# SyncE's queue in written order in the first attention stage, and the first values behind both score groups

## The chip, the cores and the metric

The kernel runs on one core of a Trainium2 chip. Such a core has a matrix engine (TensorE, PE in the profile), a vector engine (VectorE, DVE), an activation engine (ScalarE, ACT), a general engine (GpSimd, POOL) and SyncE (SP), whose queue issues the data transfers (DMAs). The metric is the time of one execution in microseconds (us) of the device. The median of three runs of the kernel before is 627.55 us (627.46 to 628.74).

## The reference

One layer of a decoder block, for 512 tokens of width 1024 and 16 learned tokens ahead of them. Two attention branches with 16 heads each read the same normalised input `u`, and a gate merges them:

```python
h = concatenate([meta_tokens, x])            # 16 + 512 rows
u = rmsnorm(h, pre_norm_g)
proj = u @ w_in                              # cq, ckv, k_pe, z_mla, fq, fk, fv, f_logit, z_fox, gate_a, gate_b
# MLA: low-rank queries and keys, 64 dimensions without and 32 with rotary position
q = rmsnorm(cq) @ w_uq;  kv = rmsnorm(ckv) @ w_ukv
o_mla = causal_attention(concat(q_nope, rope(q_pe)), concat(k_nope, rope(k_pe)), v_mla)
# FoX: plain heads of 64, logits shifted by a running sum of log forget gates
cum = cumsum(log_sigmoid(f_logit + b))
o_fox = causal_attention(fq, fk, fv, logit[t, s] += cum[t] - cum[s])
y_mla = (o_mla * silu(z_mla)) @ w_br_mla;  y_fox = (o_fox * silu(z_fox)) @ w_br_fox
mixed = (sigmoid(gate_a) * y_mla + sigmoid(gate_b) * y_fox) @ w_out
out = h + rmsnorm(mixed, post_norm_g)        # the 16 learned rows dropped
```

## The kernel before, in words

**Arithmetic.** A product of float32 operands is made of three passes on TensorE: each operand is split into a high part (cast by ScalarE, `wh` for weights) and the rest (subtracted on GpSimd or VectorE, `wl`), and high by high, high by low and low by high are summed in PSUM. So a weight must be loaded (`wload`, L120, tile `wraw`), cast and subtracted (`wsplit`, L138) before its matmuls. `wraw`, `wh` and `wl` have three buffers each, used in turn.

**Stages.** After the projections of the front, 16 attention stages follow, two heads each: FoX and MLA in turn, for pairs of heads 0 to 7 (L752). Stage 0 is FoX of pair 0, stage 1 MLA of pair 0, stage 2 FoX of pair 1. In a stage (`attention`, L640):
- `scores` (L661) makes the score matmuls into PSUM tiles `st`; there are four such banks (L475). Group 0 is the query blocks 0 to 2, group 1 is block 3. For each part VectorE adds the mask and takes the minimum (L683, out to `sf`), which also frees the bank.
- the exponentials run on ScalarE (L693), the sums and their reciprocals on VectorE (L702, L703).
- `norm` (L698) writes the probabilities as two float16 parts into `pn` (ScalarE L721, VectorE L722, GpSimd L708 to L713) and has SyncE transpose them by DMA into `pt` (L729): one transposition per block and head, of 3, 5, 7 and 9 tiles of 128.
- `values` (L734) multiplies the transposed probabilities with the values: two matmuls with `vm`, 24 with `vp`, into the tile `ov`. The first one for a head reads a part of `pt` that all four transpositions of this head write. The values of a stage are made one stage later, between that stage's score groups (`late`, L826).

**Fill.** Between these, TensorE does projections ("fills", L779 to L795): in stage 0 the gates `z` of FoX and MLA and the queries, keys and values of MLA; in stage 1 the next FoX queries `fq`, the rotary parts `ppe` of the second half of the heads, the keys `fk` and the values `v` of pair 1.

**What sets the order.** TensorE runs the attention part in the order in which it is written. In the first part of stage 0 (L808) ScalarE, VectorE and GpSimd do so too. SyncE's queue and all the rest are ordered by a scheduler when the program is built. SyncE issues one DMA after the other, and one that has to wait holds up those behind it. A unit's `make` (L199) splits its weights and asks for the loads of the next three units. The loads of stage 0 that matter here, by their names in the two programs: `fq` weights (832 before, 834 after), `ppe` weights (839, 841), `fk` weights (887, 953), FoX values' weights of pair 1 (1194, 1025), the gate `z` of stage 2 (1265, 1270). Among them stand the writing of rotated queries to DRAM (`qpe_dram`, L566) and their reading back as `QP` (L507), which waits for those writes and which the MLA scores of stage 1 need; and `CT` (L280), the forget sums for the FoX scores of the next pair.

## Time and profile before

| | before |
|---|---|
| median of 3 runs | 627.55 us |
| the profiled execution: its time | 627.48 us |
| its span, first to last instruction | 625.1 us |
| TensorE busy | 601.1 us (96%) |
| VectorE, ScalarE, GpSimd busy | 380.8, 384.7, 188.9 us |
| mean granted TensorE clock | 0.992 |
| DMA engines, time that packets took | 53.7% of 16 engines' span |

All times of the trace are counted from the start of the span. A row of a timeline has start and duration in us, the engine, the line of the kernel, the operation, the tiles out<-in, the shapes and a count; in square brackets stands how long the engine was idle before it and what ended that. "SPq" is SyncE's queue; a DMA's row there is the time that its issue took, not that of the transfer.

### The profile page before, as it was taken

The page shows a single profiled execution, that of the slowest core. Times are in us where ns is not written, and L with a number is a line of the kernel's source. Part 1 is how long each engine was busy: PE and PEld are TensorE (multiplying, and loading weights), DVE is VectorE, ACT ScalarE, POOL GpSimd, SP SyncE. Part 2 cuts the span into 40 slices and gives each one's busy share as a digit, 9 for nine tenths or more (in the row PEclk, how much of TensorE's full clock was granted, in tenths as well). Part 3 has the DMA queues.
Part 4 walks back from the last instruction along what each step waited for, and adds up shares of the span by engine and source line. Part 5 has one row for each costly group of instructions (what it writes and reads, how often), then busy time and mean ns, then how long its engine had stood idle before and what let it go on. Part 6 is the DMA issues. An engine that isn't in the chain of part 4 may idle for free.

```text
span 625.1 us, 11556 instructions
## 1 busy us (share of the span) xinstructions
PE 601.1 (96%) x4058; PEld 494.2 (79%) x4058; DVE 380.8 (61%) x1015; ACT 384.7 (62%) x838; POOL 188.9 (30%) x237
## 2 busy tenths in 40 slices
PE   3999997999999999999999999999999999999996
PEld 2879775988988989889889889887888875565885
DVE  3756566376477466565674773785977775655134
ACT  5746657388478477575774784786767754443421
POOL 3324632744425343353343444330000000003700
PEclk9999997999999999999999999999999999999998
DMA  8443577756647677557477467657253128333302
GB/s 280 130 84 91 102 164 171 187 139 152 167 109 168 164 130 149 140 138 182 102 166 180 103 159 150 159 140 201 73 157 97 46 70 266 104 102 101 102 34 102
DMA packets 204865, 85.40 MB, mean 137 GB/s; under 512 B 122684, under 2 KB 197820, under 8 KB 204808
## 3 DMA queue, kind: packets, MB, share of 16 engines
q1 hardware_dynamic: 204808, 84.67, 53.7%
q8 instruction: 32, 0.52, 0.3%
q14 instruction: 25, 0.20, 0.1%
HBM read 55.21 MB, written 4.26 MB: 95 GB/s over the span
## 4 chain that ended last, share of the span: by engine, by line
PE 92%; DVE 2%; ACT 2%; DMA 2%; SPq 1%; issue 0%; DVEq 0%; ACTq 0%
PE pg L92 14%; PE z L92 14%; PE v L92 8%; PE st L92 8%; PE fk L92 8%; PE po L92 7%; PE fq L92 7%; PE py L92 6%; PE ov L92 5%; PE yx L92 3%; PE psm L92 3%; PE mq L92 2%; PE yy L92 2%; PE vt L95 1%; PE mk L92 1%; DMA wsr<-in_w_in_dram 1%
## 5 line engine op out<-in xcount | busy, mean ns | idle before, releaser
L118 POOL TENSOR_TENSOR wl<-wraw,wh 128x1024 fp32r<-128x1024 f32 (+1 forms) x60 | 132.9, 2219 | 298.7 <-ACT wh L142 284.3
L142 ACT CAST wh<-wraw 128x1024 fp32r<-128x1024 f32 (+1 forms) x74 | 72.9, 986 | 88.0 <-issue 41.4
L693 ACT ACTIVATE sf<-sf,nb 128x144 f32<-128x144 f32 (+3 forms) x128 | 71.9, 565 | 6.1 <-DVE nb L683 6.1
L721 ACT ACTIVATE pn<-sf,ri 128x128 f16<-128x128 f32 (+3 forms) x128 | 61.9, 551 | 15.1 <-ACT sf L693 14.2
L722 DVE SCALAR_TENSOR_TENSOR pn<-sf,ri,pn 128x128 f16<-128x128 f32 (+3 forms) x128 | 65.7, 553 | 7.6 <-ACT pn L721 7.6
L92 PE MATMUL pg<-uTh,wh 128*128 128x512 f32 x128 | 51.9, 406 | 0.0
L92 PE MATMUL z<-uTh,wh 128*128 128x512 f32 x128 | 50.9, 398 | 0.0
L92 PE MATMUL z<-uTh,wl 128*128 128x512 f32 x128 | 50.1, 391 | 0.0
L92 PE MATMUL z<-uTl,wh 128*128 128x512 f32 x128 | 50.0, 391 | 0.0
L92 PE MATMUL pg<-uTh,wl 128*128 128x512 f32 x128 | 50.0, 391 | 0.0
L92 PE MATMUL pg<-uTl,wh 128*128 128x512 f32 x128 | 49.9, 390 | 0.0
L92 PE MATMUL st<-hlk,hlq 64*128 64x272 f32 (+3 forms) x480 | 48.3, 309 | 0.4 <-DVE nb L683 0.3
L683 DVE CUSTOM_DVE_ANT_0 sf<-st,maskt 128x272 f32<-128x272 f32 (+2 forms) x128 | 48.5, 435 | 0.1
L92 PE MATMUL py<-g,yw 128*128 128x512 f16 x192 | 42.6, 379 | 0.6 <-DVE yw L979 0.6
L92 PEld LDWEIGHTS st<-hlk,hlq 64*128 64x128 f32 x480 | 35.7, 187 | 6.8 <-ACT wh L142 2.5
L708 POOL TENSOR_TENSOR mt<-sf,ri 128x96 f32<-128x96 f32 (+1 forms) x32 | 9.5, 297 | 90.7 <-DVE ri L703 53.5
L92 PE MATMUL fk<-uTl,wh 128*128 128x256 f32 (+1 forms) x128 | 36.5, 285 | 0.0
L92 PE MATMUL v<-uTh,wh 128*128 128x256 f32 (+1 forms) x128 | 36.5, 285 | 0.0
L92 PE MATMUL fk<-uTh,wh 128*128 128x256 f32 (+1 forms) x128 | 36.5, 285 | 0.0
L92 PE MATMUL fk<-uTh,wl 128*128 128x256 f32 (+1 forms) x128 | 36.5, 285 | 0.0
L92 PE MATMUL v<-uTl,wh 128*128 128x256 f32 (+1 forms) x128 | 36.4, 285 | 0.0
L92 PE MATMUL v<-uTh,wl 128*128 128x256 f32 (+1 forms) x128 | 36.4, 284 | 0.0
(291 smaller groups left out, 1513.1 us busy)
## 6 DMA issues: line engine op xcount, KB each, us to landing
wraw<-in_w_in_dram SPq DMA_DIRECT2D x56, 512.0 KB, 4.5
yraw<-in_w_br_fox_dram SPq DMA_DIRECT2D x8, 512.0 KB, 6.1
yraw<-in_w_br_mla_dram SPq DMA_DIRECT2D x8, 512.0 KB, 3.6
wraw<-in_w_out_dram SPq DMA_DIRECT2D x8, 512.0 KB, 3.5
qpe_dram<-gT SPq DMA_DIRECT2D x8, 256.0 KB
pt<-pn SPq DMA_TRANSPOSE x128, 2.7
QP<-qpe_dram SPq DMA_DIRECT2D x8, 256.0 KB, 2.9
xr<-in_x_dram SPq DMA_DIRECT2D x4, 512.0 KB
```

Source lines behind the costliest of these rows:

```text
L92: nc.tensor.matmul(*a, **k)
L95: nc.tensor.transpose(*a)
L118: eng.tensor_tensor(out=lo, in0=src, in1=f32(hi), op=ALU.subtract)
L142: nc.scalar.copy(wh[:, :n], raw[:, :n])
L683: nc.vector.tensor_tensor_reduce(out=sf_of(h, b)[:, c0 : c0 + w], in0=ps[h][:, o : o + w], in1=maskt[:, m0 : m0 + w], scale=-scale, scalar ...
L693: nc.scalar.activation(sf, sf, AF.Exp, bias=sums["nb"][:, h, b : b + 1], scale=-1.0, accum_out=sums["su"][:, h, b : b + 1])
L708: nc.gpsimd.tensor_tensor(out=mt, in0=src, in1=ri.unsqueeze(3).broadcast_to([128, 2, nb_, META]), op=ALU.mult)
L721: nc.scalar.activation(hi, sf, AF.Copy, scale=rib)
L722: nc.vector.scalar_tensor_tensor(out=lo, in0=sf, scalar=rib, in1=hi, op0=ALU.mult, op1=ALU.subtract)
```

## The change

`make` can hand its loads to a list, and in stage 0 the loads that `z` of MLA asks for go on the list `lo`. Its entries (the subtraction for the MLA `z` weights and the load of the `fk` weights) are called, with the load of `QP`, among the transpositions of stage 0 behind those of block 1, where before `QP` alone was called behind those of block 0. SyncE joins the engines that run in written order, for the whole of stage 0. The loads of `CT` for pair 1, and those of stage 1's weights that are not yet loaded, are written behind the last transposition of stage 0; the keys' unit of pair 1 no longer loads `CT`. And in stage 1 alone, the values of stage 0 come behind both score groups instead of between them. The work is the same.

```diff
--- before.py
+++ after.py
@@ -196,11 +196,15 @@
         st = {}
         out = []
 
-        def make(*a):
+        def make(eng=None, later=None):
             if "w" not in st:
-                st["w"] = getw(*a)
-                for load in getattr(out[0][1], "nxt", ()):
-                    load()
+                st["w"] = getw(eng, later) if eng else getw()
+                loads = getattr(out[0][1], "nxt", ())
+                if later is None:
+                    for load in loads:
+                        load()
+                else:
+                    later.extend(loads)
 
         for i, sl in enumerate(sls):
             n = sl.stop - sl.start
@@ -270,14 +274,17 @@
     def q_fox(pr):
         return unit(f"fq{pr}", win_w(O_FQ, pr), u_act, KD, REAL, hl_done(("q", 1, pr), S, S))
 
+    def load_ct(pr):
+        for h in range(2):
+            nc.sync.dma_start(f32(CT[64 * h : 64 * h + 2, :]), c_dram[:, 2 * pr + h, :])
+
     def k_fox(pr):
         halves = hl_done(("k", 1, pr), L, HALF)
 
         def done(i, ps):
             halves(i, ps)
-            if pr and i:
-                for h in range(2):
-                    nc.sync.dma_start(f32(CT[64 * h : 64 * h + 2, :]), c_dram[:, 2 * pr + h, :])
+            if pr > 1 and i:
+                load_ct(pr)
         return unit(f"fk{pr}", win_w(O_FK, pr), u_act, KD, ALLT, done)
 
 
@@ -722,7 +729,7 @@
                             nc.vector.scalar_tensor_tensor(out=lo, in0=sf, scalar=rib, in1=hi, op0=ALU.mult,
                                                            op1=ALU.subtract)
                     for b in GRP[g]:
-                        if b == 1:
+                        if b == 2:
                             mid()
                         for h in range(2):
                             t0 = PN_STEP * (b % 3)
@@ -805,33 +812,44 @@
             fill = fills[si]
             with ExitStack() as head:
                 if si == 0:
-                    head.enter_context(tc.manual_schedule(engines={E_.PE, E_.Pool, E_.Activation, E_.DVE}))
-                    za, q, zb = early
-                    turn, rest = rope0
-                    za.make()
-                    q.make()
-                    lo = []
-                    turn()
-                    s0()
-                    zb.make(nc.vector, lo)
-                    e0({(0, 1): lambda: rest(1), (1, 1): lambda: rest(0)})
-                    s1()
-                    n0(lambda: load_qp(0))
-                    lo[0]()
-                    e1()
-                    run(fill[:4])
+                    head.enter_context(tc.manual_schedule(engines={E_.PE, E_.SP}))
+                    with tc.manual_schedule(engines={E_.PE, E_.SP, E_.Pool, E_.Activation, E_.DVE}):
+                        za, q, zb = early
+                        turn, rest = rope0
+                        za.make()
+                        q.make()
+                        lo = []
+                        turn()
+                        s0()
+                        zb.make(nc.vector, lo)
+                        e0({(0, 1): lambda: rest(1), (1, 1): lambda: rest(0)})
+                        s1()
+
+                        def between():
+                            load_qp(0)
+                            for fn in lo:
+                                fn()
+                        n0(between)
+                        e1()
+                        run(fill[:4])
                 else:
                     s0()
                     e0()
-                    for fn in late:
+                    for fn in late * (si > 1):
                         fn()
                     s1()
                     e1()
+                    for fn in late * (si == 1):
+                        fn()
                     run(fill[:4])
                     n0()
-            run(fill[4:11])
-            n1()
-            run(fill[11:])
+                run(fill[4:11])
+                n1()
+                if si == 0:
+                    load_ct(1)
+                    for _, fn in fills[1]:
+                        getattr(fn, "load", int)()
+                run(fill[11:])
             late = [va]
         run(tail[:4])
         mgates[0].make()
```

In the program that is built, the orders of TensorE, SyncE, VectorE and ScalarE differ; GpSimd's does not.

**SyncE's queue in stage 0**, from the first load of `CT` on. `pt_661` and `pt_662` are the two heads' transposed probabilities, `pn_659` group 0 and `pn_660` group 1; the changed kernel's lines here are 7 higher (L729 is L736). Before:

```order
L280 DMA CT<-c_dram 2x528
L729 DMA_TRANSPOSE pt_661<-pn_659 128x3x128
L729 DMA_TRANSPOSE pt_662<-pn_659 128x3x128
L280 DMA CT<-c_dram 2x528
L507 DMA QP<-qpe_dram 128x512
L729 DMA_TRANSPOSE pt_661<-pn_659 128x5x128
L729 DMA_TRANSPOSE pt_662<-pn_659 128x5x128
L729 DMA_TRANSPOSE pt_661<-pn_659 128x7x128
L133 DMA wraw_887<-in_w_in_dram 128x8x128
L729 DMA_TRANSPOSE pt_662<-pn_659 128x7x128
L133 DMA wraw_1194<-in_w_in_dram 128x8x128
L729 DMA_TRANSPOSE pt_661<-pn_660 128x9x128
```

After:

```order
L736 DMA_TRANSPOSE pt_661<-pn_659 128x3x128
L736 DMA_TRANSPOSE pt_662<-pn_659 128x3x128
L736 DMA_TRANSPOSE pt_661<-pn_659 128x5x128
L736 DMA_TRANSPOSE pt_662<-pn_659 128x5x128
L514 DMA QP<-qpe_dram 128x512
L133 DMA wraw_953<-in_w_in_dram 128x8x128
L736 DMA_TRANSPOSE pt_661<-pn_659 128x7x128
L736 DMA_TRANSPOSE pt_662<-pn_659 128x7x128
L736 DMA_TRANSPOSE pt_661<-pn_660 128x9x128
L736 DMA_TRANSPOSE pt_662<-pn_660 128x9x128
L279 DMA CT<-c_dram 2x528 x2
L133 DMA wraw_1025<-in_w_in_dram 128x8x128
```

The keys' weights (887, now 953) moved from behind the first transposition of 7 tiles to ahead of both; `QP` moved behind the transpositions of 5 tiles; both loads of `CT` and the values' weights (1194, now 1025) moved behind the last transposition. One more row moved, earlier on this queue: the load of the second rotary table into `gT_688` stands behind the `fq` weights (834), where before it stood ahead of the `z` weights (806).

**TensorE in stage 1, ahead of the values of stage 0.** `st` are score tiles, `vm` and `ov` the first values' operand and result. Before, the values follow the last matmuls of group 0 (400 columns wide):

```order
L92 MATMUL st_1111<-KPL,QP 128x400
L92 MATMUL st_1112<-KPL,QP 128x400
L92 LDWEIGHTS vm_666
L92 MATMUL ov_1131<-pt_661,vm_666 64x512
L92 LDWEIGHTS vm_666
L92 MATMUL ov_1131<-pt_662,vm_666 64x512
```

After, they follow the last matmuls of group 1 (256 wide), which stand directly behind those of group 0:

```order
L92 MATMUL st_1153<-KPL,QP 128x256
L92 MATMUL st_1154<-KPL,QP 128x256
L92 LDWEIGHTS vm_666
L92 MATMUL ov_1169<-pt_661,vm_666 64x512
L92 LDWEIGHTS vm_666
L92 MATMUL ov_1169<-pt_662,vm_666 64x512
```

The 20 score matmuls of group 1 moved ahead of the 26 matmuls of the values; `fq` now follows the values. On VectorE the read-outs of group 1's scores moved ahead of the gating of the values (L744), and on ScalarE the exponentials of group 1 ahead of four of the six probabilities' writes of group 0 (L721).

## The prediction

> **What bounds the kernel now.** I read the page first: TensorE is busy for 96% of the span, and its row of granted clock dips in one slice inside the run. The list of waits has one long wait of TensorE behind the front. TensorE's timeline shows it, and the table of stretches the clock in it.

> ```profile
> PE 601.1 (96%) x4058; PEld 494.2 (79%) x4058; DVE 380.8 (61%) x1015; ACT 384.7 (62%) x838; POOL 188.9 (30%) x237
> PE ov L92 <- DMA pt<-pn: 5.2, 2, 4.8
> ```

> ```profile
> 91.98 0.35 PE L92 MATMUL st<-KPL,QP 64*128 64x400 f32 x2
> 97.12 0.60 PE L92 MATMUL ov<-pt,vm 80*64 80x512 f16 x1 [4.79 <-DMA pt<-pn]
> 98.15 0.61 PE L92 MATMUL ov<-pt,vm 80*64 80x512 f16 x1 [0.42 <-DMA pt<-pn]
> 98.15 3.80 PE L92 MATMUL ov<-pt,vp 128*64 128x512 f16 x24
> ...
> 103.74 0.51 PE L92 MATMUL fq<-uTh,wh 128*128 128x512 f32 x1
> ```

> ```profile
> 92.30:96.00 3.70, 0.03 (x2) 0.00 (x0) 0.72 (x2) 2.29 (x4) 1.17 (x1) 1.00 1.20 294
> 96.00:97.10 1.10, 0.00 (x0) 0.01 (x1) 1.10 (x9) 0.88 (x4) 1.10 (x1) 0.52 1.28 288
> 97.10:102.90 5.80, 5.36 (x34) 3.74 (x36) 2.30 (x10) 4.77 (x16) 1.24 (x5) 0.50 0.65 156
> ```

> Stage 1 makes group 0's scores until 92.33; then TensorE stands 4.79 us, and 0.42 more, for the last transpositions of stage 0. From about 96.0 the clock is half, 3.7 us into the idle time, until about 102.9, so values and group 1 run slow. The chain of waits has the same pieces of the next MLA stage, without a stall:

> ```profile
> 146.64 1.97 PE ov L92 x26
> 148.60 1.42 PE st L92 x14
> 150.02 2.28 PE fq L92 x9
> ```

> Values take 148.60 - 146.64 = 1.96 us there, group 1 1.42, so about 0.7 for each of its two banks. In stage 1 the way from the end of group 0 to `fq` takes 103.74 - 92.33 = 11.41 us against 150.02 - 146.64 = 3.38. So **8.0 us** are at stake: 5.2 idle, the rest slow clock.

> Why the transpositions are late stands in SyncE's queue:

> ```profile
> 77.80 1.02 SPq L280 DMA_DIRECT2D CT<-c_dram  x1
> 78.94 4.14 SPq L729 DMA_TRANSPOSE pt<-pn  x2
> 83.21 0.35 SPq L280 DMA_DIRECT2D CT<-c_dram  x1
> 84.84 0.36 SPq L507 DMA_DIRECT2D QP<-qpe_dram  x1
> 85.27 3.88 SPq L729 DMA_TRANSPOSE pt<-pn  x3
> 89.26 0.52 SPq L133 DMA_DIRECT2D wraw<-in_w_in_dram  x1
> 89.87 1.25 SPq L729 DMA_TRANSPOSE pt<-pn  x1
> 91.22 0.53 SPq L133 DMA_DIRECT2D wraw<-in_w_in_dram  x1
> 91.83 4.12 SPq L729 DMA_TRANSPOSE pt<-pn  x2
> ```

> ```profile
> L729 SPq DMA_TRANSPOSE pt<-pn x13: 1185/1247/2856, 78.9 to 109.0; - x13
> 91.83 2.67 SPq L729 DMA_TRANSPOSE pt<-pn  x1
> 94.60 1.35 SPq L729 DMA_TRANSPOSE pt<-pn  x1
> pt<-pn SPq DMA_TRANSPOSE x128, 2.7
> ```

> An issue takes 1.25 us; two in this stretch took 2.86 and 2.67, with much data under way. The last one, issued at 94.60, lets TensorE go at 98.15, 3.55 us later (the median is 2.7).

> **The queue after the change.** Up to 78.94 the row that sets the time is the probabilities' writing, which stays. I keep 2.86 for the first issue, since the query writes ahead of it stay, and have the pair of 3 tiles end at 83.08 as before. Then come two of 5 tiles (2 x 1.29 with the gap, from 3.88 for three) to 85.7, `QP` to 86.1, the keys' weights at 86.15 (before: 89.26), and four transpositions from 86.75, the last issued at 86.75 + 3 x 1.3 = 90.65. With 3.55 us it lands at **94.2**. By the median 2.7 it would be 93.4; if each of the four issues took 2.67, the last one would start at 86.75 + 3 x 2.73 = 94.9 and land at 98.5.

> [...]

> **What holds the values then.** They are behind group 1, whose matmuls need the four score banks back. VectorE frees these in an order that starts with the MLA gate, and the gate waits on ScalarE behind the cast of the keys' weights:

> ```profile
> 93.70 1.04 ACT L142 CAST wh<-wraw 128x1024 fp32r<-128x1024 f32 x1 [4.51 <-DMA wraw<-in_w_in_dram]
> 94.65 0.59 ACT L635 ACTIVATE sil<-z 128x512 f32<-128x512 f32 x1
> 95.28 0.69 DVE L636 SCALAR_TENSOR_TENSOR sil<-sil,z 128x512 f32<-128x512 f32 x1 [5.34 <-ACT sil L635]
> ...
> 98.04 0.08 DVE L683 DVE_READ_ACCUMULATOR2_ANT nb<- 128x1 f32 x1
> ```

> The cast starts at 93.70, 4.44 us after the weights' issue, and 4.42 us after its start the last bank is free (98.12). Its place in ScalarE's order stays. So the cast starts at 86.15 + 4.44 = **90.6**; it cannot before about 90.0, since the buffer it fills is read by the gate's matmuls until then:

> ```profile
> 89.64 0.40 PE L92 MATMUL z<-uTh,wl 128*128 128x512 f32 x1
> ```

> The last bank is free at 90.6 + 4.42 = 95.0, the second bank's matmuls end at 95.7, the values (transposed at 94.2, 1.5 us before) at 95.7 + 1.96 = 97.7, and `fq` starts at **97.7** in place of 103.74.

> Does the clock stay? Even if TensorE made nothing between 92.33 and the last bank's release at 95.0, it would idle 2.7 us, and the first banks come earlier. That is under the 3.7 us above, so full clock. [...]

> The rest I cost at nothing, with these covers:

> ```profile
> 56.33 0.47 SPq L545 DMA_DIRECT2D gT<-in_rope_pe_dram  x1
> 66.41 0.39 SPq L133 DMA_DIRECT2D wraw<-in_w_in_dram  x1
> 111.05 2.42 POOL L118 TENSOR_TENSOR wl<-wraw,wh 128x1024 fp32r<-128x1024 f32 x1 [2.92 <-ACT wh L142]
> 118.54 0.29 PE L92 MATMUL v<-uTh,wh 128*128 128x272 f32 x1
> 124.87 0.27 PE L92 MATMUL st<-CT,ONE 64*128 64x144 f32 x2
> QP<-qpe_dram SPq DMA_DIRECT2D x8, 256.0 KB, 2.9
> ```

> - The rotary table goes from 56.33 to behind 66.41; its reader comes behind `ppe`, past 110. Uncovered it would be a transfer, some 4 us.
> - `CT` goes from 77.80 to about 92.1; its reader is at 124.87, or 118.8 after. `CT` had stood in front of ready work for 0.4 to 1.1 us; this is in the sum.
> - `QP` moves from 84.84 to 85.7, lands 2.9 us later at 88.6, and is read at 90.4 (`KPH,QP`). Cover 1.8 us; without it TensorE waits, us for us.
> - The values' weights of pair 1 go from 91.22 to about 92.7. Their subtraction ran at 111.05, waiting for the cast behind `fq`, for matmuls at 118.54. That order hangs on `fq`, so it moves along with 7 us of room.
> - VectorE now does group 1's read-outs before the probabilities of stage 1, whose transpositions must wait for the values' end in any case. They are read in stage 2, over 20 us later.

> **The sum** against the profiled execution: 103.74 - 97.7 = 6.0 us of the 8.0. Behind `fq` the casts wait for TensorE and not for DMAs, so the program shifts as a whole. Span 625.1 - 6.0 = 619.1; with the 2.4 us outside the span (627.48 - 625.1) that is **621.5 us**. The median of the runs is 0.07 above the profiled one: 621.5 again. If the weights land before 90.0 it gains 6.6: 620.9. If they take 2 us more: 623.5.

> **The rivals.**
> 1. *The transpositions decide.* The four of them behind the weights are issued as slowly as the one at 91.83 was. With two at 2.67, 1.42 more each, the last lands at 94.2 + 2.8 = 97.0, the values start 1.3 us later than forecast and the time is 622.8; with all four (98.5) it is 624.3, from 2.8 us more. For it: both long issues came with bulk data under way, and here `QP` and 512 KB are. Against: at 89.87 an issue right behind weights took 1.25.
> 2. *The clock drops again.* The gaps add up to a drop, and values and group 1 run at half clock: they took 103.74 - 98.15 = 5.59 for what takes 3.38, so 2.2 us are lost: 623.7. Against: no gap near 3.7 us.
> 3. *The gain is given back.* Something behind `fq` stands at an absolute time, and TensorE waits there for what it won: 627.5. This is also the case in which the order differs but semaphores hold the keys' weights where they landed before. Against: their buffer's last reader ended before 82, and the 7 us of room above.
> 4. *Slower.* TensorE now stands at group 1 with no other work, so everything hangs on the keys' weights. These stand behind `QP`, which waits for all query writes. From the cast to `fq` it is 97.7 - 90.6 = 7.1 us, so if the cast starts later than 103.74 - 7.1 = 96.6, it is a loss, us for us, and the clock's 2.2 us come on top as the idle time passes 3.7. With a cast at 98, `fq` starts at 98 + 7.1 + 2.2 = 107.3, and the time is 631. Against: `QP` was issued at 84.84, so its wait ended by then, and the writes are unchanged.

> **How the numbers follow.** Forecast (620.9 to 622.4) 0.72, rival 1 0.13, rival 2 0.05, rival 3 0.05, rival 4 0.05. The range 620.6 to 623.8 holds the forecast, half of rival 1 and rival 2, about 0.83. This kernel's measurement tells 0.2% (1.26 us) from no change; forecast and rivals 1 and 2 are faster by more: 0.90 faster, 0.05 same, 0.05 slower.

> **What would show it.** In the changed profile: `fq` of stage 1 near 97.7; the cast of the keys' weights near 90.6; group 1 of stage 1 started in pieces, each ended by VectorE's read-outs and not by a DMA; values with no wait for `pt`, 26 matmuls in about 2 us; granted clock full from 18 us to the end. I am wrong if a wait for `pt` of over 1 us stands ahead of the values (rival 1), the clock is half anywhere there (2), `fq` is early and a new wait of TensorE stands behind it (3), or the cast starts after 96 (4).

## The result

| | before | after | forecast |
|---|---|---|---|
| median of seven runs | 628.74 us (627.46 to 629.73) | 623.73 us (622.85 to 626.31) | 621.5 us |
| ratio to before (that of the two medians is 0.9920) | | 0.9931, 95% interval 0.9912 to 0.9950 | 0.9904 (621.5 / 627.55) |
| difference by the ratio | | -4.3 us (-5.5 to -3.1) | -6.0 us |
| the profiled execution: time, span | 627.48, 625.1 us | 626.31, 624.1 us | 621.5, 619.1 us |

The change makes the kernel faster, by some 70% of what was forecast. Its profiled execution is the slowest of its seven, and its span is only 1.0 us under that of before. That is the front: stage 0's scores start at 72.67 us against 71.10. In the fourteen traces of this study they start between 70.89 and 73.07, and in a second trace of the kernel before at 72.24. The three traces with SyncE's old queue have 72.06 us in the mean, the eleven with a new one 72.08, so the change has no part in it. From there to the end of group 0 in stage 1 all fourteen take 21.23 to 21.28 us. So the trace is read below from the end of group 0's scores in stage 1 (the last pair of `KPL,QP` matmuls with 400 columns) to the first `fq`; this **way** was 92.33 to 103.74, 11.41 us, before. From `fq` to the end it is 521.5 us after, 521.4 before: nothing was given back behind it.

### The profile page after: what moved, and what is told of

Its sections match the earlier page's. It is cut to its first block, busy times and chain, and to the rows that moved or that the text cites. A ratio compares the mean times of both kernels' runs of the same rounds, so it can differ in the third digit from the quotient of the medians.

```text
span 624.1 us, 11556 instructions
## 1 busy us (share of the span) xinstructions
PE 601.8 (96%) x4058; PEld 493.9 (79%) x4058; DVE 382.3 (61%) x1015; ACT 384.1 (62%) x838; POOL 188.3 (30%) x237
## 4 chain that ended last, share of the span: by engine, by line
PE 89%; ACT 4%; DMA 3%; DVE 2%; issue 1%; SPq 1%; POOL 0%; DVEq 0%; ACTq 0%
PE pg L92 14%; PE z L92 12%; PE v L92 8%; PE fk L92 8%; PE st L92 7%; PE po L92 7%; PE fq L92 7%; PE py L92 6%; PE ov L92 5%; PE yx L92 3%; PE psm L92 3%; PE yy L92 2%; PE mq L92 2%; DMA wsr<-in_w_in_dram 1%; PE vt L95 1%; PE mk L92 1%
## 5 line engine op out<-in xcount | busy, mean ns | idle before, releaser
L118 POOL TENSOR_TENSOR wl<-wraw,wh 128x1024 fp32r<-128x1024 f32 (+1 forms) x60 | 132.9, 2218 | 302.4 <-ACT wh L142 288.0
L142 ACT CAST wh<-wraw 128x1024 fp32r<-128x1024 f32 (+1 forms) x74 | 72.8, 986 | 86.6 <-issue 41.8
L729 DVE SCALAR_TENSOR_TENSOR pn<-sf,ri,pn 128x128 f16<-128x128 f32 (+3 forms) x128 | 65.7, 555 | 7.4 <-ACT pn L728 7.4
L92 PE MATMUL st<-hlk,hlq 64*128 64x272 f32 (+3 forms) x480 | 48.7, 308 | 3.5 <-DVE nb L690 3.3
L92 PE MATMUL pg<-uTh,wh 128*128 128x512 f32 x128 | 51.9, 406 | 0.0
L92 PE MATMUL z<-uTh,wh 128*128 128x512 f32 x128 | 50.9, 398 | 0.0
L92 PE MATMUL z<-uTh,wl 128*128 128x512 f32 x128 | 50.1, 391 | 0.0
L92 PE MATMUL z<-uTl,wh 128*128 128x512 f32 x128 | 50.0, 391 | 0.0
L92 PE MATMUL pg<-uTh,wl 128*128 128x512 f32 x128 | 50.0, 391 | 0.0
L92 PE MATMUL pg<-uTl,wh 128*128 128x512 f32 x128 | 49.8, 389 | 0.0
L92 PEld LDWEIGHTS st<-hlk,hlq 64*128 64x128 f32 x480 | 35.7, 185 | 10.5 <-DVE nb L690 5.0
L92 PE MATMUL py<-g,yw 128*128 128x512 f16 x192 | 42.6, 379 | 0.6 <-DVE yw L997 0.6
L92 PE MATMUL fk<-uTl,wh 128*128 128x256 f32 (+1 forms) x128 | 36.5, 286 | 0.0
L92 PE MATMUL fk<-uTh,wh 128*128 128x256 f32 (+1 forms) x128 | 36.5, 285 | 0.0
L92 PE MATMUL v<-uTh,wh 128*128 128x256 f32 (+1 forms) x128 | 36.5, 285 | 0.0
L92 PE MATMUL fk<-uTh,wl 128*128 128x256 f32 (+1 forms) x128 | 36.5, 285 | 0.0
L92 PE MATMUL v<-uTl,wh 128*128 128x256 f32 (+1 forms) x128 | 36.4, 285 | 0.0
L92 PE MATMUL v<-uTh,wl 128*128 128x256 f32 (+1 forms) x128 | 36.4, 284 | 0.0
L92 PEld LDWEIGHTS <-yw 128*128 128x128 f16 x192 | 17.9, 98 | 22.7 <-DVE yw L997 1.1
## 6 DMA issues: line engine op xcount, KB each, us to landing
qpe_dram<-gT SPq DMA_DIRECT2D x8, 256.0 KB
QP<-qpe_dram SPq DMA_DIRECT2D x8, 256.0 KB, 2.9
```

The source lines that it names most:

```text
L92: nc.tensor.matmul(*a, **k)
L118: eng.tensor_tensor(out=lo, in0=src, in1=f32(hi), op=ALU.subtract)
L142: nc.scalar.copy(wh[:, :n], raw[:, :n])
L729: nc.vector.scalar_tensor_tensor(out=lo, in0=sf, scalar=rib, in1=hi, op0=ALU.mult, op1=ALU.subtract)
```

## The profile after

The page's row of engines, and from the list of waits of the whole run two of TensorE's (us in total, times, longest):

```profile
PE 601.8 (96%) x4058; PEld 493.9 (79%) x4058; DVE 382.3 (61%) x1015; ACT 384.1 (62%) x838; POOL 188.3 (30%) x237
```

```profile
PE st L92 <- DVE nb L690: 3.3, 3, 2.8
PE ov L92 <- DMA pt<-pn: 0.2, 1, 0.2
```

The wait for `pt` (5.2 us before) is gone from this stage (the 0.2 us stand in a later one). Waits for score banks stand in its place, 2.99 of the 3.3 us here. TensorE's timeline:

```profile
93.59 0.34 PE L92 MATMUL st<-KPL,QP 64*128 64x400 f32 x2
96.72 0.39 PE L92 MATMUL st<-hlk,hlq 64*128 64x272 f32 x1 [2.79 <-DVE nb L690]
97.31 0.64 PE L92 MATMUL st<-hlk,hlq 64*128 64x272 f32 x5 [0.20 <-DVE nb L690]
99.38 0.64 PE L92 MATMUL ov<-pt,vm 80*64 80x512 f16 x2
102.65 0.50 PE L92 MATMUL fq<-uTh,wh 128*128 128x512 f32 x1
```

Group 0 ends at 93.93, so the way is 102.65 - 93.93 = 8.72 us, where 97.7 - 92.33 = 5.37 was forecast. The chain of waits shows what holds group 1 (start, length, engine and line):

```profile
88.25 5.49 DMA wraw<-in_w_in_dram
...
93.82 1.04 ACT wh L142
94.86 0.51 ACT sil L642
...
98.16 0.10 DVE nb L690
```

It is the forecast's chain: the keys' weights, their cast, the gate, the banks. The cast starts 0.11 us ahead of group 0's end, forecast were 92.33 - 90.6 = 1.73; from the cast to the last bank it is 98.26 - 93.82 = 4.44, forecast 4.42. SyncE's queue, and from the view of the tile `pt` the time of its transfers:

```profile
87.33 0.46 SPq L514 DMA_DIRECT2D QP<-qpe_dram  x1
88.25 0.39 SPq L133 DMA_DIRECT2D wraw<-in_w_in_dram  x1
88.70 8.12 SPq L736 DMA_TRANSPOSE pt<-pn  x4
```

```profile
DMA to landing us min/median/max: 2.4/2.7/4.0
```

The four issues behind the weights took 8.12 us in all, 2.03 each, where 1.3 each was forecast; the last starts at 94.77, and the longest landing, 4.0 us, is its own, so its data are there at 98.8, 4.8 us behind group 0 (1.9 were forecast, 94.2 - 92.33). The table of stretches, cut at the steps of the clock (length, then busy time of TensorE, its weight loads, VectorE, ScalarE, GpSimd, then the granted clock):

```profile
91.83:95.24 3.41, 2.10 (x30) 1.77 (x28) 0.00 (x0) 1.42 (x2) 0.81 (x3) 1.00 1.27 183
95.24:98.66 3.42, 1.63 (x17) 1.23 (x19) 3.27 (x16) 3.18 (x12) 2.05 (x1) 1.00 1.05 143
98.66:102.07 3.41, 3.41 (x25) 1.80 (x23) 2.04 (x12) 2.90 (x11) 1.32 (x4) 0.50 1.02 297
```

The clock is half for 3.41 us, although TensorE never stood for over 2.79 us, and it falls 1.9 us after work had begun again. TensorE is busy all through that window, so I estimate that half of it, 1.7 us, is lost: the 24 `vp` matmuls took 3.80 us in the kernel before, all of them at half clock, and 2.92 here, partly at half clock; "TensorE kept busy", below, has 1.80 at full clock.

## The experiments

All times by ratio to the kernel before (627.55 us), one row for each kernel. "Issues" is the time from the first to the end of the last of the four transpositions behind `QP`, "clock" the mean granted clock of the runs. Each ratio is to runs of the kernel before from the same set; there are four sets: the first row of the change, "again" to "TensorE kept busy", "keys' weights behind" to "keys' weights earlier", and the last four rows. The mean clock also counts a fall behind TensorE's last matmul, 0.3 to 3.7 us long in the fourteen traces, which costs nothing. By that I estimate that a mean of 0.995 goes with one window of 3.41 us at half clock inside the kernel, 0.992 with at least two, and 0.997 with none or one.

| kernel | ratio, 95% interval | us | way, us | issues, us | clock |
|---|---|---|---|---|---|
| before, two traces | 1 | 0 | 11.41, 12.42 | | 0.992 to 0.997 |
| the change | 0.9931 (0.9912 to 0.9950) | -4.3 | 8.72 | 8.12 | 0.994 to 0.997 |
| the change, again | 0.9942 (0.9925 to 0.9959) | -3.6 | 7.82 | 7.40 | 0.995 to 0.997 |
| values' place alone | 1.0003 (0.9990 to 1.0015) | +0.2 | 9.35 | | 0.991 to 0.997 |
| SyncE's queue alone | 0.9957 (0.9942 to 0.9973) | -2.7 | 8.41 | 7.21 | 0.992 to 0.997 |
| TensorE kept busy | 0.9923 (0.9906 to 0.9939) | -4.8 | 7.02 | 7.82 | 0.998 to 0.999 |
| keys' weights behind | 0.9971 (0.9960 to 0.9981) | -1.8 | 4.32 | 5.38 | 0.995 to 0.997 |
| cast on GpSimd | 0.9933 (0.9915 to 0.9952) | -4.2 | 8.29 | 8.33 | 0.995 to 1.0 |
| keys' weights earlier | 0.9912 (0.9895 to 0.9928) | -5.5 | 5.16 | 6.55 | 0.997 to 1.0 |
| behind, cast on GpSimd | 0.9890 (0.9873 to 0.9906) | -6.9 | 4.38 | 5.38 | 0.997 to 1.0 |
| half behind, cast on GpSimd | 0.9893 (0.9872 to 0.9914) | -6.7 | 5.61 | 6.90 | 0.997 to 1.0 |
| earlier, cast on GpSimd | 0.9899 (0.9884 to 0.9914) | -6.3 | 5.08 | 6.47 | 0.998 to 1.0 |
| behind, cast on GpSimd, values between | 0.9913 (0.9895 to 0.9931) | -5.5 | 4.52 | 5.37 | 0.995 to 0.999 |

**The two kernels, traced again.** No edit.

> The changed kernel, unaltered, a second time. The way from the end of group 0's scores of the first MLA stage to `fq` took 11.41 us before and 8.72 in the first profile of the change (102.65 - 93.93), where 5.37 was forecast. If what held it (keys' weights 5.49 us from issue to landing instead of 4.44, and one window of 3.41 us at half clock) belongs to the order, the way is 8.2 to 9.2 again, the weights take over 5 us, and the time is 4 to 5 us under before. If it was an accident of that one execution, the way is 5.4 to 6.5, the weights land after about 4.4 us, and the clock is full.

> The kernel before, unaltered, for a second trace of the same stretch. If the first trace (way from the end of group 0 to `fq` 11.41 us, two windows of 3.41 us at half clock) is typical, the way is 11 to 12 again. The timed runs of the kernel before have a mean granted clock of 0.992 to 0.994 each, so one such window fewer is possible: then the way is about 1.7 us less.

The change again, TensorE's timeline and SyncE's queue; then the kernel before again, the timelines of TensorE, SyncE's queue and ScalarE:

```profile
96.22 0.39 PE L92 MATMUL st<-hlk,hlq 64*128 64x272 f32 x1 [1.88 <-DVE nb L690]
88.91 7.40 SPq L736 DMA_TRANSPOSE pt<-pn  x4
```

```profile
99.76 0.60 PE L92 MATMUL ov<-pt,vm 80*64 80x512 f16 x1 [6.25 <-DMA pt<-pn]
90.47 0.52 SPq L133 DMA_DIRECT2D wraw<-in_w_in_dram  x1
96.44 1.04 ACT L142 CAST wh<-wraw 128x1024 fp32r<-128x1024 f32 x1 [6.07 <-DMA wraw<-in_w_in_dram]
```

The change's way is 7.82 us, a little under what "it belongs to the order" expected, and far over "an accident". The weights' cast begins 4.86 us behind their issue (5.57 in the first trace, 4.44 forecast, over 5 expected here), and one window of half clock is there again. The way before is 12.42, and there the same weights took 5.97 us from issue to cast (96.44 - 90.47), in the queue in which the first trace had 4.44; so one execution differs from another by 1 us; the means, 11.9 and 8.3, differ by 3.6 us, and so do the times.

**Each half of the change alone.** The first has the values behind both groups, the second SyncE's new queue:

```diff
# values' place alone, on the kernel before
-                    for fn in late:
+                    for fn in late * (si > 1):
...
+                    for fn in late * (si == 1):
+                        fn()
# SyncE's queue alone, on the changed kernel: these lines undone
```

> The values' new place alone; SyncE's queue as before the change. Theory A (the chain weights, cast, gate, score banks holds group 1, and each half of the change is needed): the cast stays where it was before, 1.4 us behind the end of group 0 (93.70 against 92.33), the last bank comes 4.42 later, so group 1 ends 6.5 behind group 0, the values take 1.96 more: way 8.5 at full clock, about 10.2 with one window of 3.41 us at half clock, against 11.41 before; time 1 to 3 us under before. Theory B (only the values' place matters, the queue's order does nothing): the way equals that of the whole change, 8.7, and so does the time.

> SyncE's new queue alone; the values stand between the score groups as before. Theory A (the last transposition is hardly earlier than before: 4.84 us behind the end of group 0 in the changed kernel, 98.77 - 93.93, against about 5.8 before): values wait 5 us, the clock drops, way 5.1 + 3.38 + 2.2 = 10.7, time within 1 us of before. Theory B (the transpositions were early as forecast and only the banks held the values): the last lands 1.9 us behind group 0, way 5.3, time 6 us under before.

TensorE's timelines, of the first and of the second:

```profile
97.96 0.39 PE L92 MATMUL st<-hlk,hlq 64*128 64x272 f32 x1 [3.85 <-DVE nb L683]
```

```profile
95.66 0.40 PE L92 MATMUL ov<-pt,vm 80*64 80x512 f16 x1 [2.32 <-DMA pt<-pn]
96.76 0.40 PE L92 MATMUL ov<-pt,vm 80*64 80x512 f16 x1 [0.70 <-DMA pt<-pn]
```

The values' place alone changes the wait for transpositions (4.79 and 0.42 us) into one for banks (3.85 and 0.20), and the time does not move, where theory A had 1 to 3 us. Its traced way of 9.35 looks better than its time; but that execution had a clock of 0.997, and ten of its twelve runs had 0.991 or 0.992. With a second window of 1.7 us that is 11.05, still some less than before; the rest stays open. The queue alone gains 2.7 us, more than theory A had for it and less than the 6 us of theory B: the last transposition lets TensorE go 3.42 us behind group 0 (96.76 - 93.34), against 5.82 before (98.15 - 92.33). Of the 3.6 to 4.3 us of the whole change the queue brings the most. What the values' new place adds to it, 0.9 us in this set, cannot be told from nothing (0.9942 to 0.9973 against 0.9925 to 0.9959).

**TensorE kept busy.** Ten matmuls without use into the values' bank, which is then overwritten:

```diff
+            def awake(n):
+                opo[0] = ovp.tile([128, 512], F32, tag="ov", name=f"ov{nm_}")
+                for k in range(n):
+                    mm(opo[0], uTh[:, k % KD, 0:128], uTh[:, (k + 1) % KD, 0:512], start=True, stop=True)
...
+                    if si == 1:
+                        late[0].awake(10)
                     s1()
```

> The changed kernel with ten extra matmuls of 512 columns (2.3 us, result overwritten) on TensorE between group 0 and group 1 of the first MLA stage. If the gap of 2.79 us there is what lets the clock fall, the granted clock stays full through the stage and the way to `fq` is 8.72 - 1.7 = 7.0, time 1.7 us under the changed kernel's. If the clock falls for another reason, the way stays at 8.7 and the half clock is seen again.

Its stretches by the steps of the clock:

```profile
93.48:96.89 3.41, 3.05 (x20) 2.07 (x18) 2.66 (x12) 3.17 (x11) 2.40 (x1) 1.00 1.19 176
96.89:100.31 3.42, 3.32 (x41) 2.35 (x38) 1.60 (x7) 2.91 (x11) 1.25 (x4) 1.00 0.90 238
```

The clock stays full, the way is 7.02 us as the clock theory expected, and the mean clock is 0.998 or 0.999 in each of the six runs against 0.995 in five of six. The time is 1.2 us under that of the change in the same comparison (0.9923 / 0.9942); the intervals overlap. So here the gap did let the clock fall, and it cost up to 1.7 us (8.72 - 7.02).

**The weights and the transpositions.** Two single edits on the change: the keys' weights behind all transpositions of stage 0, and their cast on another engine.

```diff
# keys' weights behind
-                            for fn in lo:
+                            for fn in lo[:-1]:
                                 fn()
...
                 if si == 0:
+                    lo[-1]()
                     load_ct(1)
# cast on GpSimd, for the keys of pair 1 alone
-        nc.scalar.copy(wh[:, :n], raw[:, :n])
+        (nc.gpsimd.tensor_copy if eng == "pool" else nc.scalar.copy)(wh[:, :n], raw[:, :n])
```

> The changed kernel with one load moved: the keys' weights behind all the transpositions of stage 0 instead of ahead of the last four. ScalarE's order changes with it: the MLA gate's activation now stands ahead of the cast of these weights. Theory T (weights under way are what slows the transpositions' issues: 3.03 and 2.05 us instead of 1.28, and what makes the last land 4.84 us behind group 0): the four issues take about 1.3 us each, the last lands 1.5 to 2.5 us behind the end of group 0; the score banks, no longer behind the weights, are all free by about 2 us behind it; way 4 to 5 us, full clock, time 3.5 to 5 us under the changed kernel. Theory Q (the transpositions slow each other, the weights have no part): the issues are slow as before, the last lands over 4 us behind group 0, the way is 6.5 to 8.5, time within 1.5 us of the changed kernel's.

> The changed kernel with the cast of the keys' weights on GpSimd instead of ScalarE, so that ScalarE's activation of the MLA gate waits for the gate's matmuls alone; SyncE's queue unaltered. Theory L (the chain weights, cast, gate, banks alone sets `fq`): banks free 2 us behind group 0, way 4.5 to 5.5, time 3 to 4 us under the changed kernel. Theory T (the transpositions are as late as the banks): group 1 ends early, then the values wait for the last transposition, 4.5 to 5 us behind group 0 (98.77 - 93.93 = 4.84 in the first trace), way 7 to 8.8 with the clock falling in that wait, time within 1 us of the changed kernel's.

Keys' weights behind: SyncE's queue, TensorE's and ScalarE's timelines, and the stretch of half clock.

```profile
88.24 5.38 SPq L736 DMA_TRANSPOSE pt<-pn  x4
94.62 0.64 PE L92 MATMUL st<-hlk,hlq 64*128 64x272 f32 x5 [0.20 <-DVE nb L690]
97.84 1.05 ACT L142 CAST wh<-wraw 128x1024 fp32r<-128x1024 f32 x1 [4.81 <-DMA wraw<-in_w_in_dram]
98.79 0.41 ACT L700 ACTIVATE sf<-sf,nb 128x144 f32<-128x144 f32 x1
110.85 0.39 PE L92 MATMUL fk<-uTh,wh 128*128 128x272 f32 x1 [3.31 <-DVE hlq L118]
112.34:115.75 3.41, 3.41 (x18) 3.41 (x17) 0.84 (x2) 0.10 (x1) 3.41 (x3) 0.50 1.08 113
```

Cast on GpSimd: SyncE's queue, TensorE's timeline, and the stretch of half clock.

```profile
87.62 8.33 SPq L736 DMA_TRANSPOSE pt<-pn  x4
96.88 0.40 PE L92 MATMUL ov<-pt,vm 80*64 80x512 f16 x1 [1.41 <-DMA pt<-pn]
97.84 0.64 PE L92 MATMUL ov<-pt,vm 80*64 80x512 f16 x1 [0.56 <-DMA pt<-pn]
97.55:100.96 3.41, 3.12 (x22) 2.09 (x23) 0.65 (x4) 3.41 (x9) 1.34 (x6) 0.50 0.90 247
```

Without the weights in front the four issues take 5.38 us, with them 7.2 to 8.3: theory T. The way falls to 4.32 us, inside its 4 to 5, at full clock. But the time is worse than that of the change, since the gain is given back: the cast, now waiting until 97.84, stands on ScalarE ahead of the exponentials, all that follows there is late, and TensorE waits 3.31 us ahead of `fk`, with a window of half clock after it. From `fq` to the end it is 526.5 us instead of 521.5. With the cast alone moved, the banks come free early and group 1 ends at 95.47; then the values wait 1.41 and 0.56 us for transpositions, the clock falls, and way and time are those of the change. So in the change the banks' chain and the transpositions end at nearly the same time, and taking away one shows the other.

**The weights four entries earlier**, behind the first two transpositions:

```diff
-                        if b == 2:
-                            mid()
+                        if b:
+                            mid(b)
...
+                        def between(b):
+                            if b == 1:
+                                lo[-1]()
+                                return
                             load_qp(0)
-                            for fn in lo:
+                            for fn in lo[:-1]:
```

> The changed kernel with the keys' weights four entries earlier, behind the first two transpositions of stage 0 and ahead of the two of 5 tiles and of `QP`. The weights are issued 3.7 us earlier (about 84.6 instead of 88.25), so the cast is no longer bound by them but by its buffer, read until 1.5 to 2.4 us ahead of group 0's end. Theory L: last bank 2 to 3 us behind group 0, way 5 to 6, 3 us under the changed kernel. Theory T (the same 512 KB slow the transpositions wherever they are ahead of some): the pair of 5 tiles is issued slowly and the last transposition still lands 3 to 5 us behind group 0; way 6 to 8.5, within 2 us of the changed kernel's. A loss would come from `QP`, later by that slowing: its reader in group 0 would wait.

SyncE's queue, ScalarE's and TensorE's timelines:

```profile
87.29 6.55 SPq L736 DMA_TRANSPOSE pt<-pn  x4
90.14 1.05 ACT L142 CAST wh<-wraw 128x1024 fp32r<-128x1024 f32 x1 [0.65 <-PE z L92]
93.04 0.39 PE L92 MATMUL st<-hlk,hlq 64*128 64x272 f32 x1 [0.42 <-DVE nb L690]
```

The cast starts 2.49 us ahead of group 0's end (92.63) and waits for its buffer, read by `z`, no longer for the load. So the way is 5.16 us and the clock full, as theory L has it, and the time is 1.2 to 1.9 us under that of the change, with overlapping intervals, and less than its 3. The last four issues are slower than without weights (6.55 against 5.38), which is theory T's share, and `QP` harmed nothing.

**Both edits, and their halves.** The weights behind (or half of them, or earlier) with the cast on GpSimd; and the first of these with the values back between the groups. The edits are those above; for the half, the load is two DMAs of four slices each:

```diff
+                    nc.sync.dma_start(st["r"][:, 0:4], src[:, 0:4])
...
+                nc.sync.dma_start(st["r"][:, 4:8], src[:, 4:8])
```

(In the next texts the 3.94 us of the load alone is counted from 94.42, the end of group 1's first matmul, 94.03 + 0.39; from the end of group 0, as in the table, it is 4.32. Their 8.05 and 5.1 us for the four issues leave out the gaps between these, some 0.3 us; the table has 8.33 and 5.38.)

> Both edits: the keys' weights behind all transpositions of stage 0, and their cast on GpSimd. With the load alone moved, `fq` came 3.94 us behind the end of group 0, but the cast, later by 4 us, stood on ScalarE ahead of the exponentials and held them up; TensorE then waited 3.31 us ahead of `fk` for `hlq`, with a window of half clock behind it, and `fq` to the end took 526.5 us instead of 521.3. Theory (ScalarE's order is the whole of that loss): way 4 us again, no wait ahead of `fk`, `fq` to the end 521.0 to 521.6, time 619.5 to 621.5, 7 us under the kernel before. Rival (the weights themselves are too late for `fk`): the wait ahead of `fk` stays at 2 to 4 us and the time over 624.

> The cast on GpSimd, and the keys' weights' load in two: the first 256 KB where the change has the load, the other 256 KB behind all transpositions. With all of it in front the last transposition landed 4.75 us behind the end of group 0, with none at most 2.3. If the data in front is what slows the transpositions, in proportion: about 3.5 us, the sum of the four issues about 6.5 us (8.05 with all, 5.1 with none), way 5.5 to 6. If one long load in front costs the same whatever its size: 4.5 to 5 us and way 7 to 8.5.

> The keys' weights four entries earlier, and their cast on GpSimd. With the early load alone `fq` came 5.16 us behind group 0's end, with 0.62 us of waits for score banks and 0.42 for the last transposition. If the cast on ScalarE still holds the gate there (it began 2.5 us ahead of group 0's end), the bank waits fall under 0.3 us and the values wait 0.5 to 1.2 us for the transposition instead: way 4.8 to 5.2, time within 1 us of the early load alone (622.3). If taking the cast off ScalarE gives more than the transposition allows, the way falls to 4.2.

> As the kernel with both edits, but the values of stage 0 back between the score groups. The last transposition then lands about 2 us behind group 0. If the values' new place is worth something once the transpositions are on time, TensorE waits 1.5 to 2.3 us ahead of the values and the way is 5 to 5.7 against 4: 1 to 1.7 us slower than with the values behind. If it is worth nothing, way and time agree within 0.5 us.

In this order: the first kernel's SyncE queue, and its row in the table of stretches from 90 us to its `fq`; the second's SyncE queue; TensorE's timeline for the third, and for the fourth, with a row of its list of waits:

```profile
87.36 5.38 SPq L736 DMA_TRANSPOSE pt<-pn  x4
```

```profile
90.00:97.60 7.60, 7.30 (x81) 5.68 (x80) 5.92 (x29) 5.69 (x19) 1.91 (x3) 1.00 1.07 227
```

```profile
88.42 6.90 SPq L757 DMA_TRANSPOSE pt<-pn  x4
```

```profile
96.70 0.40 PE L92 MATMUL ov<-pt,vm 80*64 80x512 f16 x1 [0.36 <-DMA pt<-pn]
```

```profile
93.30 0.40 PE L92 MATMUL ov<-pt,vm 80*64 80x512 f16 x1 [0.81 <-DMA pt<-pn]
```

```profile
PE fk L92 <- DVE hlq L118: 0.8, 1, 0.8
```

- Both edits: TensorE works 7.30 of 7.60 us from 90 us to `fq`, there is no wait ahead of `fk`, 521.6 us from `fq` to the end, 621.08 us, the best kernel here: 2.6 to 3.3 us under the change (0.9890 against 0.9931 and 0.9942, from different sets; the intervals do not meet). The two variants that follow cannot be told from it in time.
- Half the data in front: 6.90 us of issues, between 5.38 and 8.33, and a way of 5.61, inside the 5.5 to 6 expected if the slowing goes with the amount of data. It is one trace, and that proportion is not shown: with all 512 KB in front the issues took from 7.21 to 8.33 us, and the last transposition let TensorE go 3.65 us behind group 0 here (97.24 - 93.59), between the 3.42 of SyncE's queue alone and the 4.80 of the cast on GpSimd (97.84 - 93.04), which both have 512 KB in front.
- Earlier and on GpSimd: bank waits of 0.20 us, 0.36 us for a transposition, way 5.08. The cast on ScalarE cost the earlier load next to nothing; the times cannot be told apart.
- Values between the groups: the last transposition lets TensorE go 1.15 us behind group 0 (93.30 - 92.15), and the way is 4.52, equal within 0.5 us to that with the values behind. The time is 1.4 us more, with overlapping intervals, and 0.81 us of it is a wait ahead of `fk`. Once the transpositions are on time, the values' place is worth little in the way, and nothing in time that can be told apart.

## Why the prediction was right and wrong

- **What bounds it, and at what price: right.** The wait for the last transpositions and the slow clock were the cost, and SyncE's order the cause: its queue alone gains 2.7 us, the values' place alone nothing. With both edits the kernel takes 621.08 us, about what was forecast for the change, 6.9 us of the 8.0 at stake.
- **The chain that holds the values: right in kind.** Weights, cast, gate, banks, 4.44 us from the cast to the last bank against 4.42, values at once behind group 1. `QP`, `CT`, the rotary table and the values' weights cost nothing that shows: 21.26 us from stage 0's scores to the end of group 0 against 21.23, and 521.5 us from `fq` to the end against 521.4, so nothing was given back either.
- **"The cast starts at 86.15 + 4.44": a mis-sized term.** Counted from group 0's end, the cast came 1.62 us later than forecast in the first trace (0.11 against 1.73 ahead), 0.71 in the second (93.31 against 94.33, 1.02 ahead). Of the 1.62, about 0.5 is the issue (88.25 is 5.68 ahead of group 0's end, forecast 6.18: a pause of 0.46 us between `QP`'s issue and the weights'), and the rest the landing, 5.49 us. The same pause of 0.46 to 0.47 us stands behind `QP` in all nine traces in which `QP` is issued within 0.2 us of the transpositions of 5 tiles, whether the weights or a transposition come next, and 0.07 us in the other five, where `QP` is issued later behind the row ahead of it; so it is no wait of the weights for something of their own, and its cause stays open. I took 4.44 from one trace as if it were a constant, and for another place in the queue: with the weights between `QP` and the last four transpositions, five traces have 4.86 to 5.64 us from their issue to the cast (5.35 in the mean). For the same load the runs show 4.15 us (93.67 to 97.82, behind all transpositions) to 5.97 (the kernel before again). In the change `QP` is read right ahead of it and transpositions follow at once; whether either of them slows it was not tried.
- **"No gap near 3.7 us, so full clock": the step that failed.** In the first trace the clock fell behind two windows with 2.10 and 1.63 us of TensorE work, in the second behind two with 2.35 and 2.30, though no wait was over 2.79 us. The window at half clock cost an estimated 1.7 us in each (half of 3.41). The two errors are the whole of the miss: 8.72 - 5.37 = 3.35 is 1.62 + 1.73, and 7.82 - 5.37 = 2.45 is 0.71 + 1.74; where TensorE was kept busy, the cast was 1.51 late (92.65 against a group 0 end of 92.87) and 7.02 - 5.37 = 1.65 is 1.51 + 0.14. Rival 2 had this at 0.05, with a price of 2.2 us. I read a threshold of 3.7 us off one idle time that was longer, 4.79 us: counted back from the fall at 96.05, that idle time was one whole window of 3.41 us without work (the first row below) and 0.31 us ahead of it, from 92.33 to 92.64. That the clock falls only behind such an idle window was not shown: in the change it fell behind one with 1.63 us of work. From the kernel before:

```profile
92.64:96.05 3.41, 0.00 (x0) 0.00 (x0) 0.77 (x2) 2.29 (x4) 1.22 (x1) 1.00 1.21 292
96.05:99.47 3.42, 1.93 (x9) 0.82 (x11) 2.15 (x13) 3.14 (x12) 1.13 (x1) 0.50 1.16 280
```

- **"Four transpositions at 1.3 each": wrong, and covered.** They took 8.12 us instead of 5.2. That was rival 1 (0.13) in its first case, two at 2.67, which makes 5.2 + 2.8 = 8.0. It hid behind the late banks: the cast on GpSimd shows that without the late banks the transpositions would have set the end, with waits of 1.41 and 0.56 us behind group 1. The runs show the transpositions held up by the data in front, and already in their issues: these took 5.38, 6.90 and 7.21 to 8.33 us with 0, 256 and 512 KB in front, so 512 KB cost them 1.8 to 3.0 us.
- **The number, in part luck.** The median, 623.73 us, lies just inside the range of 620.6 to 623.8, at the end that was kept for rivals 1 and 2, and not in the 620.9 to 622.4 that had the chance of 0.72. By the ratio the time missed by 1.7 us, the way by 2.45 and 3.35. The forecast counted from a way of 11.41 us, and the second trace of the kernel before has 12.42; as far as two traces tell, the longer way before hid a part of the miss.
- **Rivals 3 and 4** did not come in the change. Rival 3 came in an experiment, by a way that I had not seen: ScalarE ran in its order, with a late cast (4.81 us of wait, to 97.84) ahead of ready work.

## What to carry over

A load that was moved ahead of transpositions on SyncE's queue slowed them here (their four issues took 7.21 to 8.33 us with it directly in front, 5.38 without), and its own landing time was no constant (4.15 to 5.97 us from issue to cast): one trace gives one sample of it, for one place in the queue. When two chains end close together, a removed wait shows the other chain, so price both, and look at what a late operand blocks on the engine that waits for it in order. A longest wait of 1.88 or 2.79 us was no guarantee for the clock here, in the two traces of the change: count TensorE's work over the 7 us around it (the falls came behind 6.83 us with 2.59 to 4.86 of work).

## What the runs showed of the hardware that I had not expected

```profile
91.99:95.40 3.41, 2.35 (x31) 2.01 (x30) 0.52 (x1) 2.09 (x4) 1.71 (x3) 1.00 1.46 216
95.40:98.81 3.41, 2.30 (x22) 1.65 (x24) 3.14 (x17) 3.17 (x13) 1.39 (x1) 1.00 0.72 154
98.81:102.23 3.42, 3.42 (x27) 1.98 (x23) 2.00 (x10) 2.91 (x10) 1.39 (x5) 0.50 1.12 324
```

- Two windows together fit all the falls that were seen: the eight falls inside the kernels came behind pairs with 2.59 to 4.86 us of work in 6.83, and no fall behind pairs with 5.44 or more. At the ends of the fourteen traces, where TensorE runs out of work, the clock fell behind pairs with up to 4.90 us (4.75 in the kernel before, 4.57 in the change) and did not behind one with 5.02. This was not tested by a run of its own.
- GpSimd cast 128x1024 values in 1.15 us in the kernel with both edits, ScalarE in 1.04 in the mean (64 casts of the kernel before).
